# Four branch products of a decoder layer, eight half products each, rewritten as seven in Strassen's form

## The chip, the cores and the metric

One Trainium2 chip, one core. The time is the device time of one execution of the whole kernel in microseconds. TensorE is called PE, VectorE DVE, ScalarE ACT, GpSimd Pool, and the queue that issues most transfers SP, as the profile does.

## What is computed

One decoder layer on 1024 tokens with 1024 features. A norm and one wide input projection feed four branches: forgetting attention, a linear recurrence, stick-breaking attention and attention into a memory of 256 tokens. What this case is about comes after them:

```python
branches = jnp.stack([y_fox, y_lru, y_sb, y_mem], axis=2).astype(x.dtype)
gates = jax.nn.sigmoid(proj("gates").reshape(b, s, N_BRANCH, D_MODEL) + b_gate[l])
projected = jnp.einsum('bsnc,ncd->bsnd', branches, w_branch[l])
mixed = jnp.sum(gates * projected, axis=2)
x = x + mixed @ w_out[l]
```

Each branch has its own 1024 x 1024 weight; the four products of 1024 x 1024 x 1024 are gated, summed to `mixed`, and go through `w_out`. A gated MLP follows. All of it is float32.

## The kernel before, in words

**Precision.** PE multiplies in a rounded float32 format (F32R). So every operand is split in a high part (an ACT cast, line 131) and a low part (source minus high part, a DVE `tensor_tensor`, line 132, function `split`), and each product is three matmuls: high by high, high by low, low by high (`mm3`, lines 184 to 191). A matmul takes a 128 x 128 weight tile and a 128 x 512 operand.

**Before the branch products.** Norm and projections, the recurrence, then the attention stage, in which PE alternates between attention and a filler of projections by a planner's costs (lines 555 to 952). The filler's last work are the gate projections; they read the normed input `hTh`, `hTl` (64 KB of each partition) to their end, and their raw results go to DRAM (`gate_d`, without the sigmoid). The branches' results `y_d` lie in DRAM too. In the fox part of that stage Pool makes a sum of two 128 x 1024 tiles once per head (`fd`, line 745), and DVE splits projection weights there with line 132; in the stick-breaking part Pool masks 128 x 128 blocks with `affine_select` (line 832).

**The branch products (lines 957 to 1007).** The order is 1, 3, 0, 2 (recurrence, memory, fox, stick-breaking). For each branch the eight 128-row strips of `y_d[b]` are loaded (line 981) and split into twelve slots, so that strips of the next branch come in while this one is multiplied; the slots of the first branch lie outside the space of `hTh` and `hTl`. For every pair of output strips 256 columns of the weight are loaded and split by `load_w` (lines 210 to 228). For every output strip `m` the gate is loaded (line 990) and put through a sigmoid on ACT (line 991), 48 matmuls fill a PSUM tile of 128 x 1024, and DVE multiplies it by the gate (line 999 or 1001) and, from the second branch on, adds it to `mixed[m]` (line 1002). In the last branch `mixed[m]` is split at once (line 1005). Pool has nothing to do here.

**After.** The output projection takes the parts of `mixed` as weights, in 128 x 256 matmuls (lines 1018 to 1036), then the MLP.

The program is written in order, and a scheduler settles the order on every engine's queue and all waits; each engine and SP work their queues in order.

Of the kernel before, what the change touches and what calls it, by code (L numbers as in the profile page):

```python
# [7 lines left out]
F32 = mybir.dt.float32  # L8
F32R = mybir.dt.float32r
AF = mybir.ActivationFunctionType  # L10
ALU = mybir.AluOpType
AX = mybir.AxisListType
PSUM = bass.MemoryType.PSUM
DRAM = bass.MemoryType.DRAM

P = 128
S = 1024
D = 1024
KT = D // P
# [43 lines left out]
def build(tc, a, out):  # L63
    nc = tc.nc
# [17 lines left out]
    gate_d = dp.tile([4, D, S], F32, name="gate_d")  # L82
    y_d = dp.tile([4, D, S], F32, name="y_d")
# [46 lines left out]
    def split(src, hi, lo):  # L130
        nc.scalar.copy(hi, src)  # L131
        nc.vector.tensor_tensor(lo, src, hi, op=ALU.subtract)  # L132
# [42 lines left out]
    def pe(ins):  # L175

        if prev:
            tc.add_manual_dep(ins.ins, prev.pop().ins.name, NOSYNC, reason="order")
        prev.append(ins)
# [4 lines left out]
    def mm3(ps, pairs, pe=None):  # L184

        n = len(pairs)
        for i, (wh, wl, xh, xl) in enumerate(pairs):
            for j, (l, r) in enumerate(((wh, xh), (wh, xl), (wl, xh))):
                ins = nc.tensor.matmul(ps, l, r, start=(i == 0 and j == 0), stop=(i == n - 1 and j == 2))  # L189
                if pe:  # L190
                    pe(ins)
# [4 lines left out]
    pp = tc.alloc_tile_pool(name="psA", bufs=1, space=PSUM, reuse_waits="tile")  # L196
    hp = tc.alloc_tile_pool(name="hp", bufs=1, reuse_waits="tile")
    wp = tc.alloc_tile_pool(name="wp", bufs=2, side="right", reuse_waits="tile")
# [11 lines left out]
    def load_w(pool, src, n, step=None, gain=None):  # L210


        wh = pool.tile([P, KT, n], F32R, tag="wh", name="wh", bufs=2)
        wl = pool.tile([P, KT, n], F32R, tag="wl", name="wl", bufs=2)
        rk = 1024 // n
        for k0 in range(0, KT, rk):
            wr = pool.tile([P, rk, n], F32, tag="wr", name="wr", bufs=WRB)
            nc.sync.dma_start(wr, src[k0 * P:(k0 + rk) * P, :].rearrange("(k p) n -> p k n", p=P))
            if gain is not None:
                for k in range(rk):  # L220
                    g, h = gain[:, k0 + k:k0 + k + 1], wh[:, k0 + k, :]
                    nc.scalar.activation(h, wr[:, k, :], AF.Identity, scale=g)
                    nc.vector.scalar_tensor_tensor(wl[:, k0 + k, :], wr[:, k, :], g, h, op0=ALU.mult, op1=ALU.subtract)
                continue
            for k in range(0, rk, step or rk):
                ks, kd = slice(k, k + (step or rk)), slice(k0 + k, k0 + k + (step or rk))
                split(wr[:, ks, :], wh[:, kd, :], wl[:, kd, :])
        return wh, wl
# [22 lines left out]
    with ExitStack() as s1:  # L251
# [5 lines left out]
        def next_w(src, raw=None):  # L257
            wpools.reverse()
            return load_w512(wpools[1], src, raw)
# [108 lines left out]
        for name, base in (("fq", C_FQ), ("fk", C_FK), ("fv", C_FV), ("sv", C_SV), ("mq", C_MQ)):  # L368
            for c in range(0, D, 512):
                w = w_first if (name == "fq" and c == 0) else next_w(w_in[:, base + c:base + c + 512])  # L370
# [17 lines left out]
    with ExitStack() as s1:  # L388
# [77 lines left out]
        for c in range(KT):  # L466
# [3 lines left out]
            nxt = lru_in(c + 1) if c + 1 < KT else None  # L470
# [7 lines left out]
    with ExitStack() as s1:  # L478
# [3 lines left out]
        pp = s1.enter_context(tc.tile_pool(name="psA2", bufs=1, space=PSUM, reuse_waits="tile"))  # L482
# [433 lines left out]
        while vi < len(vq):  # L916
            now = clock["pe"] - (HOPF if vq[vi][0] in fox else HOP)
            if vi < ti:
                n, jp = vq[vi]
# [11 lines left out]
            if ti < len(vq) and ti - vi < PHB and slots["T"][-BANKS[1]] <= now:  # L931
                n, jp = vq[ti]
# [4 lines left out]
            if si < len(sq) and slots["S"][-BANKS[0]] <= now:  # L937
                n, f = sq[si]
# [15 lines left out]
    hp.release()  # L954


    pp = tc.alloc_tile_pool(name="psB", bufs=1, space=PSUM, reuse_waits="tile")
    xp = tc.alloc_tile_pool(name="xp", bufs=1, reuse_waits="tile")
    mixed = [xp.tile([P, S], F32, tag="x%d" % k, name="mixed") for k in range(KT)]
    ya = tc.alloc_tile_pool(name="ya", bufs=1, reuse_waits="tile")  # L960
    yb = tc.alloc_tile_pool(name="yb", bufs=1, side="right", reuse_waits="tile")

    def y_slot(g, k):
        n = (8 * g + k + 4) % 12
        pool = ya if n < 8 else yb
        return (pool.tile([P, S], F32R, tag="h%d" % n, name="yh"), pool.tile([P, S], F32R, tag="l%d" % n, name="yl"))

    def mmb():
        return pp.tile([P, 2, 512], F32, tag="up", name="mmb", bufs=3)

    def Tb():
        return pp.tile([P, 512], F32, tag="dn", name="T", bufs=2)

    order = (1, 3, 0, 2)
    mhl = []
    for g, b in enumerate(order):
        ys = {}
        ko = [4, 5, 6, 7, 0, 1, 2, 3] if g == 0 else list(range(KT))
        for k in ko:
            yr = yb.tile([P, S], F32, tag="yr", name="yr", bufs=2)  # L980
            nc.sync.dma_start(yr, y_d[b, k * P:(k + 1) * P, :])
            hl = y_slot(g, k)
            split(yr, *hl)
            ys[k] = hl
        for m in range(KT):
            if m % 2 == 0:
                w = load_w(wp, a["w_branch"][0, b, :, m * P:m * P + 256], 256)
            off = (m % 2) * P
            gt = yb.tile([P, S], F32, tag="gt", name="gt", bufs=2)
            nc.sync.dma_start(gt, gate_d[b, m * P:(m + 1) * P, :])  # L990
            nc.scalar.activation(gt, gt, AF.Sigmoid)
            ps = mmb()
            for half in range(2):
                sl = slice(half * 512, half * 512 + 512)
                mm3(ps[:, half], [(w[0][:, k, off:off + P], w[1][:, k, off:off + P], ys[k][0][:, sl], ys[k][1][:, sl])
                                  for k in ko])
            ps = ps.rearrange("p a n -> p (a n)")
            if g == 0:
                nc.vector.tensor_tensor(mixed[m], ps, gt, op=ALU.mult)
            else:  # L1000
                nc.vector.tensor_tensor(gt, ps, gt, op=ALU.mult)
                nc.vector.tensor_tensor(mixed[m], mixed[m], gt, op=ALU.add)
            if g == 3:
                hl = y_slot(4, m)
                split(mixed[m], *hl)
                mhl.append(hl)
    yb.release()

    hp = tc.alloc_tile_pool(name="h2", bufs=1, side="right", reuse_waits="tile")
    h2h = hp.tile([P, KT, S], F32R, name="h2h")  # L1010
# [9 lines left out]
    for t0 in (0, 4):  # L1020
        for c in range(0, D, 256):
            w = load_w(wp, a["w_out"][0, :, c:c + 256], 256)
            for t in range(t0, t0 + 4):
                sl = slice(t * P, (t + 1) * P)
                ps = mmb()[:, 0, :256]
                mm3(ps, [(mhl[k][0][:, sl], mhl[k][1][:, sl], w[0][:, k, :], w[1][:, k, :]) for k in range(KT)],
                    pe if c + 256 == D or turns else None)
                if len(turns) > 1 or (turns and c + 256 < D and t > t0):
                    turns.pop(0)(pe)
                    if not turns:  # L1030
                        prev.clear()
                nc.vector.tensor_tensor(x2[t][:, c:c + 256], x2[t][:, c:c + 256], ps, op=ALU.add)
                if c + 256 == D:
                    turns.append(norm_T(np_, Tb, x2[t], None, h2h, h2l, t * P, 1, mmb().rearrange("p a n -> p (a n)")))
# [17 lines left out]
    for p in range(NFF // 2):  # L1052
# [3 lines left out]
        al = tp.tile([P, 2, S], F32R, tag="al", name="al", bufs=2)  # L1056
        for f in range(2):
            n = 2 * p + f
# [10 lines left out]
        wh = tp.tile([P, 2, D], F32R, tag="dh", name="wdh")  # L1069
        wl = tp.tile([P, 2, D], F32R, tag="dl", name="wdl")  # L1070
        for f in range(2):
            wr = tp.tile([P, D], F32, tag="dr", name="wdr", bufs=2)
            nc.sync.dma_start(wr, wd[(2 * p + f) * P:(2 * p + f + 1) * P, :])
            split(wr, wh[:, f], wl[:, f])
        for t in range(NT):
            ts = slice(t * P, (t + 1) * P)
            for half in range(2):
                sl = slice(half * 512, half * 512 + 512)
                ps = pp.tile([P, 512], F32, tag="dn", name="dn", bufs=2)
# [4 lines left out]
    tp.release()  # L1084
    pp.release()
    hp.release()
    wp.release()
    xp.release()
    edge.release()
    es.close()  # L1090

# [25 lines left out]
```

## Time and profile before

| | us |
|---|---|
| median of 3 runs (2983.04 to 2988.02) | 2984.13 |
| the profiled execution's own time | 2983.88 |
| its span, from the first instruction to the last | 2982.2 |
| the stretch of the branch products, first to last matmul's start | 1799.42 to 2152.21 |
| end of the last split of `mixed` | 2158.46 |

The span lies inside the time of the same execution; the 1.7 us between them are around the program. Positions in the trace are counted from the span's start. "Granted clock" is TensorE's, 1.00 being 2.4 GHz. A matmul's duration in the trace is longer than the distance to the next one, as matmuls overlap; what a row of matmuls takes is read from their starts.

### The profile page before, as it was taken

To read this page: it belongs to the slowest core of one execution; us is meant where nothing else is said; L and a number is where in the kernel's file an instruction comes from. 1 tells how busy PE (TensorE), PEld (TensorE's weight loads), DVE (VectorE), ACT (ScalarE), POOL (GpSimd) and SP (SyncE) were. 2 spreads that over 40 slices of the span, in tenths; PEclk is the share of its full clock that TensorE was granted. 3 is DMA by queue.
4 is the path that set the end of the run, shared out by engine and by line. 5 is a ranking of instruction groups with operands and counts; after the bars stand their busy time and mean duration, and the time that the engine had idled before them with its cause. 6 is when DMAs were issued, how large, how long until landed. Compare 5 with 4: busy or idle time off the path is not lost. (4 is left out here: it accounts for less than half of the span.)

```text
span 2982.2 us, 38824 instructions
## 1 busy us (share of the span) xinstructions
PE 2913.9 (98%) x14800; PEld 2461.8 (83%) x14800; DVE 1737.7 (58%) x3261; ACT 1270.0 (43%) x2264; POOL 301.9 (10%) x502
## 2 busy tenths in 40 slices
PE   8999999999999999999999999999999999999999
PEld 6878888887888888888887888888898888888887
DVE  8564325556657877878888873443445444444443
ACT  5333223578346666666666662322234222222221
POOL 0000000000312122224433320000000000000000
PEclk9999999999999999999999999999999999999999
DMA  6345543212766566644444534443422111111101
GB/s 214 127 142 183 184 146 122 71 57 62 268 196 184 170 161 161 165 123 135 119 128 120 133 121 162 145 159 113 139 88 85 43 52 48 43 43 57 57 29 57
DMA packets 210922, 358.77 MB, mean 120 GB/s; under 512 B 14816, under 2 KB 141824, under 8 KB 206640
## 3 DMA queue, kind: packets, MB, share of 16 engines
q1 hardware_dynamic: 189744, 267.49, 27.8%
q0 software_dynamic: 20992, 88.79, 11.3%
q8 instruction: 117, 1.92, 0.3%
q14 instruction: 69, 0.57, 0.1%
HBM read 255.50 MB, written 100.73 MB: 119 GB/s over the span
## 5 line engine op out<-in xcount | busy, mean ns | idle before, releaser
L182 PE MATMUL mm<-hTl,wh 128*128 128x512 f32 x768 | 304.9, 397 | 0.0
L182 PE MATMUL mm<-hTh,wh 128*128 128x512 f32 x768 | 304.2, 396 | 0.7 <-DVE fs L589 0.7
L182 PE MATMUL mm<-hTh,wl 128*128 128x512 f32 x768 | 304.1, 396 | 0.0
L132 DVE TENSOR_TENSOR wl<-wr,wh 128x1024 fp32r<-128x1024 f32 (+1 forms) x216 | 209.5, 998 | 111.3 <-ACT wh L131 111.0
L189 PE MATMUL up<-h2h,wl 128*128 128x512 f32 x704 | 274.2, 389 | 0.0
L189 PE MATMUL up<-h2h,wh 128*128 128x512 f32 x704 | 274.1, 390 | 0.0
L189 PE MATMUL up<-h2l,wh 128*128 128x512 f32 x704 | 273.9, 389 | 0.0
L189 PE MATMUL mm<-wh,hTh 128*128 128x512 f32 x640 | 255.2, 399 | 2.2 <-ACT hTh L131 2.2
L131 ACT CAST wh<-wr 128x1024 fp32r<-128x1024 f32 (+1 forms) x216 | 176.7, 865 | 179.5 <-PE mmb L189 75.4
L189 PE MATMUL mm<-wh,hTl 128*128 128x512 f32 x640 | 251.3, 393 | 0.2 <-DVE hTl L132 0.2
L189 PE MATMUL mm<-wl,hTh 128*128 128x512 f32 x640 | 250.5, 391 | 0.0
L614 DVE TENSOR_TENSOR pl<-T,ph 128x512 fp32r<-128x512 f32 (+1 forms) x336 | 203.1, 632 | 66.8 <-ACT ph L613 65.8
L613 ACT CAST ph<-T 128x512 fp32r<-128x512 f32 (+1 forms) x336 | 172.7, 553 | 133.1 <-PE T L851 119.7
L182 PE MATMUL S<-kx,qq 128*128 128x512 f32 (+2 forms) x768 | 196.7, 357 | 8.5 <-DVE mx L802 7.2
L189 PE MATMUL mmb<-yh,wh 128*128 128x512 f32 x512 | 198.3, 390 | 2.7 <-ACT yh L131 2.7
L189 PE MATMUL mmb<-yl,wh 128*128 128x512 f32 x512 | 199.2, 390 | 0.3 <-DVE yl L132 0.3
L189 PE MATMUL mmb<-yh,wl 128*128 128x512 f32 x512 | 198.6, 389 | 0.0
L1081 DVE TENSOR_TENSOR x<-x,dn 128x512 f32<-128x512 f32 x176 | 119.9, 687 | 101.7 <-PE dn L189 101.7
L851 PE MATMUL T<-ident,pr 128*128 128x128 f32 x1152 | 162.4, 277 | 14.1 <-DVE pr L837 14.1
L834 DVE TENSOR_TENSOR_SCAN gm<-gm 128x128 f32<-128x128 f32 (+7 forms) x128 | 171.5, 1358 | 7.7 <-POOL gm L832 7.6
L182 PE MATMUL PV<-pl,vx 128*128 128x256 f32 (+1 forms) x640 | 159.8, 288 | 14.2 <-DVE pl L614 14.1
L182 PEld LDWEIGHTS mm<-hTh,wh 128*128 128x128 f32 x768 | 145.1, 189 | 26.4 <-DVE fs L589 1.1
(270 smaller groups left out, 6342.3 us busy)
## 6 DMA issues: line engine op xcount, KB each, us to landing
wr<-in_w_in_dram SPq DMA_DIRECT2D x104, 512.0 KB, 4.6
wr<-in_w_up_dram SPq DMA_DIRECT2D x44, 512.0 KB, 3.5
qq<-fq_d POOLq DMA_DIRECT2D x32, 512.0 KB, 7.1
gate_d<-gs SPq DMA_DIRECT2D x64, 256.0 KB, 2.4
qq<-sq_d POOLq DMA_DIRECT2D x32, 512.0 KB, 5.1
wr<-in_w_branch_dram SPq DMA_DIRECT2D x32, 512.0 KB, 4.8
yr<-y_d SPq DMA_DIRECT2D x32, 512.0 KB, 4.2
gt<-gate_d SPq DMA_DIRECT2D x32, 512.0 KB, 3.9
```

Source lines behind the costliest of these rows:

```text
L131: nc.scalar.copy(hi, src)
L132: nc.vector.tensor_tensor(lo, src, hi, op=ALU.subtract)
L182: pe(nc.tensor.matmul(*args, **kw))
L189: ins = nc.tensor.matmul(ps, l, r, start=(i == 0 and j == 0), stop=(i == n - 1 and j == 2))
L613: nc.scalar.copy(ph[:, :n], t[:, :n])
L614: nc.vector.tensor_tensor(pl[:, :n], t[:, :n], ph[:, :n], op=ALU.subtract)
L834: nc.vector.tensor_tensor_scan(gm[:, 0:w][:, ::-1], gm[:, 0:w][:, ::-1], gm[:, 0:w][:, ::-1], 1.0, op0=ALU.mult, op1=ALU.min)
L851: pe(nc.tensor.transpose(t[:, n * P:(n + 1) * P], self.prs[qi][:, j * P:(j + 1) * P], ident))
L1081: nc.vector.tensor_tensor(x2[t][:, sl], x2[t][:, sl], ps, op=ALU.add)
```

## The change

Per branch the weight and the branch's result are cut in halves both ways: `a11` to `a22` are 512 x 512 quarters of the weight (features by inputs), `b11` to `b22` of `y_d[b]` (inputs by tokens). Seven half products of 512 x 512 x 512 are made, 48 matmuls each: a11 b11, a12 b21, s1 t1, s2 t2, s4 b22, s3 t3 and a22 t4, where s1 to s4 and t1 to t4 are eight sums of quarters, made on Pool on tiles of 128 x 2048 (most of them in place of a quarter). Each product's two operands are split into parts just one product ahead (`prep`), in two buffers each: four casts on ACT and four 128 x 1024 subtractions on DVE per product. PSUM holds two sets of four banks, `al` and `be`; products that share a sum accumulate in one bank, and in between three of the seven are copied out by ACT (`kept`). `take` loads a 128 x 512 gate, puts it through the sigmoid, adds the copy to the bank on DVE, multiplies by the gate on DVE and adds to `mixed` on Pool (on DVE for the last product of the last branch). The raw quarters lie in `ya`, which is now where `hTh` and `hTl` were, and in `yb`; `mixed` moves to the other side of SBUF. Loads are four weight quarters and four quarters of `y_d`, 1 MB each, per branch, and 16 gates of 256 KB. For the next branch, a11 and b11 are asked for after the fourth product, a12 and b22 after the fifth, the other four after the sixth.

The diff, cut to its core:

```diff
+    xp = tc.alloc_tile_pool(name="xp", bufs=1, side="right", reuse_waits="tile")
+    ya = tc.alloc_tile_pool(name="ya", bufs=1, reuse_waits="tile")
+    yb = tc.alloc_tile_pool(name="yb", bufs=1, reuse_waits="tile")
+    def add(out_, a_, b_, op):
+        nc.gpsimd.tensor_tensor(out_, a_, b_, op=op)
+    LA, LB = (0, 1, 2, 3, 8), (4, 5, 6, 7, 9)
+    def parts(pool, src, tag):
+        h = pool.tile([P, 4, 512], F32R, tag=tag + "h", name=tag + "h", bufs=2)
+        l = pool.tile([P, 4, 512], F32R, tag=tag + "l", name=tag + "l", bufs=2)
+        for k in (0, 2):
+            split(src[:, k:k + 2], h[:, k:k + 2], l[:, k:k + 2])
+        return h, l
+    def prep(a_, b_):
+        return parts(wp, a_, "w") + parts(yb, b_, "y")
+    def product(bank, ops, first):
+        wh, wl, yh, yl = ops
+        for q in range(4):
...
+            for k in range(4):
+                for j, (l, r) in enumerate(((wh, yh), (wh, yl), (wl, yh))):
+                    nc.tensor.matmul(ps, l[:, k, fs], r[:, k], start=(first and k == 0 and j == 0),
+                                     stop=(k == 3 and j == 2), skip_group_check=not first)
+            yield q, ps
+    def take(g, q, i, l, ps, part):
+        gt = yb.tile([P, 512], F32, tag="gt", name="gt", bufs=5)
+        nc.sync.dma_start(gt, gate_d[b, m * P:(m + 1) * P, sl])
+        nc.scalar.activation(gt, gt, AF.Sigmoid)
+        if part is not None:
+            nc.vector.tensor_tensor(part, part, ps, op=ALU.add)
+            ps = part
+        if g == 0:
+            nc.vector.tensor_tensor(mixed[m][:, sl], ps, gt, op=ALU.mult)
+        else:
+            nc.vector.tensor_tensor(gt, ps, gt, op=ALU.mult)
+            eng = nc.vector if g == 3 and i == 1 and l == 0 else nc.gpsimd
+            eng.tensor_tensor(mixed[m][:, sl], mixed[m][:, sl], gt, op=ALU.add)
...
+    for g, b in enumerate(order):
+        add(s1, r["a21"], r["a22"], ALU.add)
+        add(t1, r["b12"], r["b11"], ALU.subtract)
+        cur, ops = ops, prep(r["a12"], r["b21"])
+        p1 = [kept(ps, "p1") for q, ps in product("al", cur, True)]
+        add(s3, r["a11"], r["a21"], ALU.subtract)
+        add(s2, s1, r["a11"], ALU.subtract)
+        add(t2, r["b22"], t1, ALU.subtract)
+        cur, ops = ops, prep(s1, t1)
+        for q, ps in product("be", cur, True):
+            take(g, q, 0, 0, ps, p1[q])
+        add(s4, r["a12"], s2, ALU.subtract)
+        add(t3, r["b22"], r["b12"], ALU.subtract)
+        cur, ops = ops, prep(s2, t2)
+        x5 = [kept(ps, "x5") for q, ps in product("be", cur, True)]
+        add(t4, r["b21"], t2, ALU.subtract)
+        cur, ops = ops, prep(s4, r["b22"])
+        u2 = [kept(ps, "u2") for q, ps in product("al", cur, False)]
+        cur, ops = ops, prep(s3, t3)
+        for q, ps in product("be", cur, False):
+            take(g, q, 0, 1, ps, u2[q])
+        cur, ops = ops, prep(r["a22"], t4)
+        for q, ps in product("al", cur, False):
+            take(g, q, 1, 1, ps, x5[q])
+        cur = ops
+        if b1 is not None:
+            ops = prep(nxt["a11"], nxt["b11"])
+        for q, ps in product("al", cur, False):
+            take(g, q, 1, 0, ps, None)
+            if b1 is None:
+                mixed_parts(4 + q)
-    yb = tc.alloc_tile_pool(name="yb", bufs=1, side="right", reuse_waits="tile")
...
-        for m in range(KT):
-            if m % 2 == 0:
-                w = load_w(wp, a["w_branch"][0, b, :, m * P:m * P + 256], 256)
-            off = (m % 2) * P
-            gt = yb.tile([P, S], F32, tag="gt", name="gt", bufs=2)
-            nc.sync.dma_start(gt, gate_d[b, m * P:(m + 1) * P, :])
-            nc.scalar.activation(gt, gt, AF.Sigmoid)
...
-            if g == 0:
-                nc.vector.tensor_tensor(mixed[m], ps, gt, op=ALU.mult)
-            else:
-                nc.vector.tensor_tensor(gt, ps, gt, op=ALU.mult)
-                nc.vector.tensor_tensor(mixed[m], mixed[m], gt, op=ALU.add)
```

`mixed_parts` splits a strip of `mixed` as line 1005 did; strips 0 to 3 after the fifth product of the last branch, 4 to 7 after the last product's quarters. In the first branch (`g == 0`) nothing is added to `mixed`.

## Rows read from the trace of the kernel before

**Rows 1.** The page's first part: busy time, share of span, instructions.

```profile
span 2982.2 us, 38824 instructions
PE 2913.9 (98%) x14800; PEld 2461.8 (83%) x14800; DVE 1737.7 (58%) x3261; ACT 1270.0 (43%) x2264; POOL 301.9 (10%) x502
```

**Rows 2.** Stretches: length, each engine's busy time and instructions, granted clock, DMA.

```profile
0.00:10.00 10.00, 1.38 (x7) 1.41 (x8) 2.37 (x9) 3.97 (x6) 3.21 (x11) 1.00 0.83 239
10.00:20.00 10.00, 7.89 (x26) 5.62 (x25) 8.58 (x17) 7.82 (x13) 0.00 (x0) 1.00 1.01 404
...
1799.40:2152.40 353.00, 350.03 (x1537) 287.38 (x1536) 143.35 (x121) 99.73 (x98) 0.00 (x0) 1.00 0.43 139
```

**Rows 3.** Timeline, PE, at the start of the branch products.

```profile
1799.19 0.39 PE L182 MATMUL mm<-hTh,wl 128*128 128x512 f32 x1
1799.42 0.39 PE L189 MATMUL mmb<-yh,wh 128*128 128x512 f32 x1
...
1801.91 0.39 PE L189 MATMUL mmb<-yh,wl 128*128 128x512 f32 x1
```

**Rows 4.** Groups by line of the same stretch, costliest first.

```profile
L189 PE MATMUL mmb<-yl,wh 128*128 128x512 f32 x512 | 199.2, 390 | 0.3 <-DVE yl L132 0.3
...
L189 PE MATMUL mmb<-yh,wh 128*128 128x512 f32 x512 | 198.3, 390 | 2.7 <-ACT yh L131 2.7
...
L132 DVE TENSOR_TENSOR wl<-wr,wh 128x1024 fp32r<-128x1024 f32 x32 | 38.6, 1218 | 12.0 <-ACT wh L131 12.0
...
L131 ACT CAST yh<-yr 128x1024 fp32r<-128x1024 f32 x28 | 29.0, 1049 | 37.0 <-DMA yr<-y_d 33.9 <-PE mmb L189 3.0
```

**Rows 5.** Timeline, DVE: two splits in a run; the last split of `mixed`.

```profile
1826.94 2.36 DVE L132 TENSOR_TENSOR wl<-wr,wh 128x1024 fp32r<-128x1024 f32 x2 [0.36 <-ACT wh L131]
...
2157.24 1.22 DVE L132 TENSOR_TENSOR yl<-mixed,yh 128x1024 fp32r<-128x1024 f32 x1
```

**Rows 6.** Groups by line, whole span: Pool's sum, and ACT on 128 x 512.

```profile
L745 POOL TENSOR_TENSOR fd<-fb,mask 128x1024 f32<-128x1024 f32 x16 | 38.6, 2409 | 87.4 <-DMA fb<-fb_d 68.1 <-DVE sm L821 13.7 <-DVE mx L671 5.7
...
L811 ACT ACTIVATE gm<-S 128x512 f32<-128x512 f32 x80 | 48.7, 609 | 39.7 <-DVE pr L837 26.1 <-PE S L182 8.1 <-POOL pr L832 4.4
```

**Rows 7.** Timeline, DVE then Pool, around the Pool sum at 934.89.

```profile
934.97 0.69 DVE L614 TENSOR_TENSOR pl<-T,ph 128x512 fp32r<-128x512 f32 x1 [0.65 <-ACT ph L613]
935.58 2.27 DVE L132 TENSOR_TENSOR wl<-wr,wh 128x512 fp32r<-128x512 f32 x1
...
934.89 2.40 POOL L745 TENSOR_TENSOR fd<-fb,mask 128x1024 f32<-128x1024 f32 x1 [6.01 <-DMA fb<-fb_d]
```

**Rows 8.** Timeline, DVE then Pool, around the Pool sum at 1159.19.

```profile
1160.33 3.62 DVE L132 TENSOR_TENSOR wl<-wr,wh 128x512 fp32r<-128x512 f32 x4 [0.40 <-ACT wh L131]
...
1159.19 2.40 POOL L745 TENSOR_TENSOR fd<-fb,mask 128x1024 f32<-128x1024 f32 x1 [6.17 <-DMA fb<-fb_d]
```

**Rows 9.** Line 132 from 900 to 1290: shortest, median, longest in ns.

```profile
L132 DVE TENSOR_TENSOR wl<-wr,wh x32: 672/682/2268, 935.6 to 1254.5; 128x512 fp32r<-128x512 f32 x32
```

**Rows 10.** Timeline, DVE then Pool, 1342 to 1347.

```profile
1342.61 0.77 DVE L132 TENSOR_TENSOR wl<-wr,wh 128x512 fp32r<-128x512 f32 x1
1343.30 1.21 DVE L837 TENSOR_TENSOR pr<-pr,gm 128x1023 f32<-128x1023 f32 x1
1344.44 1.88 DVE L132 TENSOR_TENSOR wl<-wr,wh 128x512 fp32r<-128x512 f32 x3
1346.24 0.68 DVE L614 TENSOR_TENSOR pl<-T,ph 128x512 fp32r<-128x512 f32 x1
...
1342.80 3.67 POOL L832 TENSOR_SCALAR_AFFINE_SELECT pr<-pr 128x128 f32<-128x128 f32 x1
1346.43 0.28 POOL L832 TENSOR_SCALAR_AFFINE_SELECT gm<-gm 128x128 f32<-128x128 f32 x1
```

**Rows 11.** DMA issues: size of each, median us from issue to landing.

```profile
wr<-in_w_branch_dram SPq DMA_DIRECT2D x32, 512.0 KB, 4.8
gt<-gate_d SPq DMA_DIRECT2D x32, 512.0 KB, 3.9
```

More of the change, by code (lines that the diff above doesn't have):

```diff
@@ L954, in build @@
     hp.release()
-    pp = tc.alloc_tile_pool(name="psB", bufs=1, space=PSUM, reuse_waits="tile")
-    xp = tc.alloc_tile_pool(name="xp", bufs=1, reuse_waits="tile")
+    pp = tc.alloc_tile_pool(name="psW", bufs=1, space=PSUM, reuse_waits="tile")
+    xp = tc.alloc_tile_pool(name="xp", bufs=1, side="right", reuse_waits="tile")
     mixed = [xp.tile([P, S], F32, tag="x%d" % k, name="mixed") for k in range(KT)]
     ya = tc.alloc_tile_pool(name="ya", bufs=1, reuse_waits="tile")
-    yb = tc.alloc_tile_pool(name="yb", bufs=1, side="right", reuse_waits="tile")
@@ L963, in y_slot, with raw @@
[L963 to L966, printed above, removed]
+    yb = tc.alloc_tile_pool(name="yb", bufs=1, reuse_waits="tile")
+    def raw(n, name):
+        return (ya if n < 8 else yb).tile([P, 4, 512], F32, tag="r%d" % n, name=name)
+    def add(out_, a_, b_, op):
+        nc.gpsimd.tensor_tensor(out_, a_, b_, op=op)
+    LA, LB = (0, 1, 2, 3, 8), (4, 5, 6, 7, 9)
@@ new lines, in load_a, with load_b @@
+    def load_a(b, i, j, slot):
+        t = raw(LA[slot], "wr%d%d" % (i, j))
+        nc.sync.dma_start(t, a["w_branch"][0, b, j * 512:(j + 1) * 512, i * 512:(i + 1) * 512].rearrange(
+            "(k p) n -> p k n", p=P))
+        return t
+    def load_b(b, j, l, slot):
+        t = raw(LB[slot], "yr%d%d" % (j, l))
+        nc.sync.dma_start(t, y_d[b, j * 512:(j + 1) * 512, l * 512:(l + 1) * 512].rearrange("(k p) n -> p k n", p=P))
+        return t
+    def parts(pool, src, tag):
[4 more added lines that the diff above has]
+        return h, l
@@ new lines, in prep @@
+    def prep(a_, b_):
[3 more added lines that the diff above has]
+        for q in range(4):
+            fs = slice(q * P, (q + 1) * P)
+            if first:
+                banks[bank, q] = pp.tile([P, 512], F32, tag="%s%d" % (bank, q), name=bank)
+            ps = banks[bank, q]
+            for k in range(4):
[3 more added lines that the diff above has]
+            yield q, ps
@@ new lines, in build, with kept @@
+    banks = {}
+    order = (1, 3, 0, 2)
+    mhl = [None] * KT
+    def kept(ps, name):
+        t = yb.tile([P, 512], F32, tag="ev", name=name, bufs=8)
+        nc.scalar.copy(t, ps)
+        return t
+    def take(g, q, i, l, ps, part):
+        b, m, sl = order[g], q + 4 * i, slice(l * 512, (l + 1) * 512)
+        gt = yb.tile([P, 512], F32, tag="gt", name="gt", bufs=5)
[10 more added lines that the diff above has]
+            eng.tensor_tensor(mixed[m][:, sl], mixed[m][:, sl], gt, op=ALU.add)
@@ new lines, in mixed_parts, with first_loads @@
+    def mixed_parts(m):
+        pair = mhl[m // 2 * 2]
+        if m % 2 == 0:
+            pair = (ya.tile([P, 2, S], F32R, tag="r%d" % MT[m // 2][0], name="mh"),
+                    ya.tile([P, 2, S], F32R, tag="r%d" % MT[m // 2][1], name="ml"))
+        split(mixed[m], pair[0][:, m % 2], pair[1][:, m % 2])
+        mhl[m] = pair
+    MT = ((0, 4), (1, 7), (2, 5), (3, 6))
+    def first_loads(b):
+        return {"a11": load_a(b, 0, 0, 0), "b11": load_b(b, 0, 0, 0)}
+    nxt = first_loads(order[0])
@@ new lines, in build @@
+    nxt.update(a12=load_a(order[0], 0, 1, 1), b21=load_b(order[0], 1, 0, 2))
+    nxt.update(a21=load_a(order[0], 1, 0, 2), a22=load_a(order[0], 1, 1, 3))
+    nxt.update(b12=load_b(order[0], 0, 1, 1), b22=load_b(order[0], 1, 1, 3))
+    ops = prep(nxt["a11"], nxt["b11"])
+    for g, b in enumerate(order):
+        r, nxt = nxt, {}
+        b1 = order[g + 1] if g < 3 else None
+        s1 = raw(LA[4], "s1")
+        add(s1, r["a21"], r["a22"], ALU.add)
+        t1 = raw(LB[4], "t1")
+        add(t1, r["b12"], r["b11"], ALU.subtract)
+        cur, ops = ops, prep(r["a12"], r["b21"])
+        p1 = [kept(ps, "p1") for q, ps in product("al", cur, True)]
+        s3, s2 = r["a21"], r["a11"]
+        add(s3, r["a11"], r["a21"], ALU.subtract)
+        add(s2, s1, r["a11"], ALU.subtract)
+        t2 = r["b11"]
+        add(t2, r["b22"], t1, ALU.subtract)
+        cur, ops = ops, prep(s1, t1)
+        for q, ps in product("be", cur, True):
+            take(g, q, 0, 0, ps, p1[q])
+        s4, t3 = r["a12"], r["b12"]
+        add(s4, r["a12"], s2, ALU.subtract)
+        add(t3, r["b22"], r["b12"], ALU.subtract)
+        cur, ops = ops, prep(s2, t2)
+        x5 = [kept(ps, "x5") for q, ps in product("be", cur, True)]
+        t4 = r["b21"]
+        add(t4, r["b21"], t2, ALU.subtract)
+        cur, ops = ops, prep(s4, r["b22"])
+        u2 = [kept(ps, "u2") for q, ps in product("al", cur, False)]
+        if b1 is not None:
+            nxt = first_loads(b1)
+        cur, ops = ops, prep(s3, t3)
+        for q, ps in product("be", cur, False):
+            take(g, q, 0, 1, ps, u2[q])
+        if b1 is not None:
+            nxt.update(a12=load_a(b1, 0, 1, 1), b22=load_b(b1, 1, 1, 3))
+        else:
+            for m in range(4):
+                mixed_parts(m)
+        cur, ops = ops, prep(r["a22"], t4)
+        for q, ps in product("al", cur, False):
+            take(g, q, 1, 1, ps, x5[q])
+        if b1 is not None:
+            nxt.update(b21=load_b(b1, 1, 0, 2), a21=load_a(b1, 1, 0, 2), a22=load_a(b1, 1, 1, 3),
+                       b12=load_b(b1, 0, 1, 1))
+        cur = ops
+        if b1 is not None:
+            ops = prep(nxt["a11"], nxt["b11"])
+        for q, ps in product("al", cur, False):
+            take(g, q, 1, 0, ps, None)
+            if b1 is None:
+                mixed_parts(4 + q)
@@ L968, in mmb @@
+    yb.release()
+    pp.release()
+    pp = tc.alloc_tile_pool(name="psB", bufs=1, space=PSUM, reuse_waits="tile")
     def mmb():
@@ L972, in Tb @@
         return pp.tile([P, 512], F32, tag="dn", name="T", bufs=2)
[L974 to L984, printed above, removed]
-        for m in range(KT):
-            if m % 2 == 0:
-                w = load_w(wp, a["w_branch"][0, b, :, m * P:m * P + 256], 256)
-            off = (m % 2) * P
-            gt = yb.tile([P, S], F32, tag="gt", name="gt", bufs=2)
-            nc.sync.dma_start(gt, gate_d[b, m * P:(m + 1) * P, :])
-            nc.scalar.activation(gt, gt, AF.Sigmoid)
[L992 to L997, printed above, removed]
-            if g == 0:
-                nc.vector.tensor_tensor(mixed[m], ps, gt, op=ALU.mult)
-            else:
-                nc.vector.tensor_tensor(gt, ps, gt, op=ALU.mult)
-                nc.vector.tensor_tensor(mixed[m], mixed[m], gt, op=ALU.add)
[L1003 to L1007, printed above, removed]
     hp = tc.alloc_tile_pool(name="h2", bufs=1, side="right", reuse_waits="tile")
@@ L1025, in build @@
                 ps = mmb()[:, 0, :256]
-                mm3(ps, [(mhl[k][0][:, sl], mhl[k][1][:, sl], w[0][:, k, :], w[1][:, k, :]) for k in range(KT)],
+                mm3(ps, [(mhl[k][0][:, k % 2, sl], mhl[k][1][:, k % 2, sl], w[0][:, k, :], w[1][:, k, :]) for k in range(KT)],
                     pe if c + 256 == D or turns else None)
@@ L1086, in build @@
     hp.release()
+    xp.release()
     wp.release()
-    xp.release()
     edge.release()
```

## The prediction

> **What bounds the kernel now.** I began with the page: PE is busy for 98% of the span, DVE for 58%, ACT for 43%, Pool for 10% [rows 1]. The table by stretches then says the same of the 353.0 us of the branch products: PE 350.0, DVE 143.4, ACT 99.7, Pool nothing at all, granted clock 1.00 [rows 2]. The list of groups by line gives the matmuls, three kinds of 512 each, 1536 in all [rows 4]. Their 0.39 us are overlapped; the timeline has eleven steps from 1799.42 to 1801.91, so one matmul takes 2.49 / 11 = 0.2264 us [rows 3]. 1536 x 0.2264 = 347.8 us: the stretch is matmuls back to back, with 5 us of stops. It begins with no pause behind the last gate matmul, which reads hTh [rows 3], and its last consequence, the last split of `mixed`, ends at 2157.24 + 1.22 = 2158.46 [rows 5]. From 1799.4 that is **359.1 us**, the figure that I set the new stretch against. The rest of the program is unchanged, so the sum is made on the profiled execution's own 2983.88 us, which is 0.25 below the median of the runs shown. Some 0.2% (6 us) is what a measurement of this kernel can tell from no change.
>
> **The change, part by part.**
>
> *PE.* 4 branches x 7 products x 48 = 1344 matmuls of the same shape: 192 fewer, worth 192 x 0.2264 = **43.5 us**, and 304.3 us are left. This is the whole gain, and it comes only if PE stays the bound.
>
> *DVE.* Parts used to be made once per operand strip, 16 splits of 128 x 1024 per branch. Now they are made per product: 7 x 2 x 2 = 28 per branch. In a run one takes 2.36 - 1.22 = 1.14 us [rows 5], so 112 x 1.14 = 127.7 us. A `take` with a kept copy costs an addition from PSUM and a multiplication by the gate, 12 per branch, at 128 x 512: in a run of three such splits, (1.88 - 0.68) / 2 = 0.60 us each [rows 10]. The multiplications with both operands in SBUF come to 48 x 0.60 = 28.8; the instructions that read a bank (48 additions and the 16 multiplications of the seventh products) to 38.4. The last branch has four additions to `mixed` (2.4) and eight splits of it (9.1). All told 206 us: by itself under PE's 304.
>
> *Pool.* Sums of 128 x 1024 took 2.41 us on average and 2.40 in the two that I follow below [rows 6 to 8]. Of 128 x 2048 and 128 x 512 the trace has none; I take 2.40 per 1024 in proportion. The other end is a fixed part as large as Pool's shortest mask, 0.28 [rows 10]: then a long sum is 0.28 cheaper and a short one (2.40 + 0.28) / 2 - 1.20 = 0.14 dearer, 32 x 0.28 - 44 x 0.14 = 3 us less in all. Eight sums of 2048 per branch are 64 units; additions to `mixed`, 16 quarters in the second and third branch and 12 in the last, are 22: 86 x 2.40 = **206.4 us**, also under 304. GPSIMD Engine Reference of the Trainium skill, section 3.1, gives 4497 ns for an addition of N = 2048 in float32, where proportion gives 4.80; by it the sum below would be 32 x 0.30 = 9.7 us less, near 3028; no run here shows that length.
>
> *DVE and Pool together.* Each fits beside PE, but the trace shows that they don't fit beside one another. At 934.89 Pool begins a sum and holds until 937.29. DVE, with a bank as one of its sources, isn't touched (0.69 us). Its next instruction is a split of `wl` from `wr` and `wh`, both in SBUF: started at 935.58, it takes 2.27 us and ends 0.56 after Pool's sum [rows 7]. The median of that instruction in the same stage is 0.682, and 2.268 is the longest of 32 [rows 9]. It happens again at 1159.19: four splits take 3.62 us where 0.68 + 3 x 0.60 = 2.48 is usual, 1.14 more, and Pool's sum still had 1.26 to run [rows 8]. So a DVE instruction with two SBUF sources does nothing while a Pool sum runs. The other way round too: a Pool mask of 0.28 us takes 3.67 us, while DVE runs five such instructions one behind the other, and it ends just after a DVE instruction with a bank as its source has begun [rows 10]. Splits, the multiplications of kept copies and the additions to `mixed` are all of this kind, and so are the Pool sums. They are one queue: 127.7 + 28.8 + 2.4 + 9.1 + 206.4 = **374.4 us**, against 304.3 of PE. Per branch it is 57.6 + 31.9 + 7.2 = 96.7 us in the second and third, against 76.1 of PE.
>
> *What the queue can't fill.* The operand buffers are two, so the parts of product n + 1 can't be begun before product n - 1 is done, and each time a cast of 1.05 us [rows 4] stands ahead of the first split. In that time the queue may be empty: between 0 and 28 x 1.05 = 29.4 us. I take 29.4, as no code prepares anything further ahead, and some parts wait for Pool's sum as well.
>
> *The start.* The raw quarters now lie in the space of hTh and hTl, free only at 1799.4; the first branch's slots used not to. Two loads of 1 MB at the best rate shown, 404 GB/s, are 5.2 us [rows 2], and a 512 KB load lands in 4.8 [rows 11], of which its bytes are 1.3 at that rate, so 3.5 are latency. a11's first split can begin at 3.5 + 2.6 + 1.05 = 7.2 us; b11 lands at 8.7, and its first cast and split end at 10.9, when the first matmul starts. For the common queue I take 9 us, between the two; bounds 6 and 14, the latter if the loads run at half that rate. The other six quarters land behind, 2.6 us each, while the queue works.
>
> *What is hidden.* ACT per branch: 28 casts x 1.05, and 28 copies and sigmoids at 0.61 [rows 6] make 46.5 of at least 76. DMA moves the same 12 MB per branch (a mean share of 0.43 in the stretch before [rows 2]), and SP issues 24 transfers per branch as before. The last four loads stand in the queue ahead of the seventh product's four gates (10.4 us at 404 GB/s, and 3.9 to land [rows 11]); these are wanted two products later, so I charge 0, at most 5 us at each of three branch ends, and only if PE is the bound. Copies (`kept`) and the first matmuls of the output projection cost nothing: the former are behind other products, the latter run on strips 0 to 3 until the last split, the same chain (multiply, add, cast, split) as before; bound +6. The clock was 1.00 even in the first 10 us, with PE busy for 1.38 [rows 2]; I charge nothing for PE's new waits.
>
> **Sum.** 9 + 374.4 + 29.4 = 412.8 us to the last split, against 359.1: +53.7. 2983.88 + 53.7 = 3037.6, so **3038 us**. With the empty time at 0, the start at 6 and Pool's fixed part, it would be 2983.9 + 53.7 - 29.4 - 3 - 3 = 3002.
>
> **The rivals.**
>
> *PE stays the bound (faster).* For it: only two DVE splits met a Pool sum in this trace, both of 128 x 512; nobody saw a queue of both. Against it: both were held to the Pool sum's end to within 0.6 us. If they ran side by side, the stretch would be 11 + 304.3 + 6.1 for the tail (2152.4 to 2158.5) + the 5 us of stops of before = 326, 33 less: 2951. This decides if the port is held for so little of a Pool sum that the common queue falls under PE's time: (304 - 168) / 206, two thirds of its duration. Chance 0.12. If the part held is a little above this, the time passes through no change on its way to 3038: 0.04.
>
> *Who goes first (slower still).* In rows 10 DVE kept the port through five instructions. If Pool does the same with s3, s2 and t2 in a row (14.4 us) and s4, t3 (9.6), DVE stands still with the split at its head, and the additions from banks behind it don't run beside Pool any more: up to 38.4 more, 3038 to 3076. If the two take turns instead, Pool gets in after every split, and the same bound holds. Rows 10 speak against turns: Pool asked at 1342.80, and four more DVE instructions went ahead. It decides from the point at which two Pool sums are ready at once. Chance 0.12. SBUF — State Buffer of the Trainium skill, section "Who interferes with whom", has the exclusive hold too and says that issue order decides who blocks; by that rule it would be turns, and this trace does not agree on that part.
>
> *The saving isn't there.* That the change does not drop 192 matmuls can be set aside: the loops of the diff give 48 per product and seven products per branch, without a condition.
>
> **How the numbers follow.** The forecast has 0.72, the rival of turns 0.12, side by side 0.12, between 0.04. Faster by over 0.2%: 0.13; within: 0.04; slower: 0.83. The range runs from 2996, the first case with every bound at its low end (3002) and a measurement's grain of 6 under it, to 3080, the second at its end (3076) with most of the tail's bound; it leaves out side by side, the case between and little more.
>
> **What would show it.** Right: PE stops for 5 to 20 us in products that wait for s1, s2, s4 or their parts; 128 x 1024 splits with 2 to 6 us among ones of 1.22; DVE and Pool together near full through the stretch; 1344 matmuls at 0.226. Wrong: splits at 1.22 throughout beside Pool sums, PE busy share near 95% in the stretch and its length near 320. A stop of about 11 us at 1799 is there in either case.

## The result, and the profile after

The changed kernel takes 3050.98 us (median of 4 runs, 3049.19 to 3054.01) against 2983.59 for the kernel before: ratio 1.0226, 95% interval 1.0208 to 1.0243. It is slower by 67 us (62 to 73); 54 were forecast. The profiled execution took 3054.01, 70.1 more than that of before.

The page of the changed kernel, its first part:

```profile
span 3052.2 us, 38870 instructions
PE 2897.8 (95%) x14608; PEld 2441.1 (80%) x14608; DVE 1930.1 (63%) x3369; ACT 1342.7 (44%) x2392; POOL 551.0 (18%) x578
```

192 matmuls are gone, as said, and the span is 70 us longer: PE now waits. Against [rows 1] DVE is busy for 192 us more and Pool for 249 more. The table of stretches shows where (columns as in [rows 2]); the bounds are the last gate matmul, the four branches' ends in round figures, and the tail:

```profile
1799.40:1809.30 9.90, 0.04 (x1) 0.04 (x1) 2.42 (x3) 3.63 (x5) 0.00 (x0) 0.74 0.95 316
1809.30:1906.00 96.70, 75.08 (x288) 58.83 (x288) 79.66 (x42) 41.94 (x54) 56.41 (x11) 0.85 0.47 169
1906.00:1998.00 92.00, 79.73 (x336) 64.52 (x336) 80.55 (x57) 42.14 (x56) 51.45 (x16) 0.95 0.41 137
1998.00:2102.00 104.00, 83.15 (x336) 67.40 (x336) 85.07 (x56) 41.69 (x56) 71.04 (x24) 0.89 0.36 122
2102.00:2219.00 117.00, 96.04 (x387) 77.49 (x388) 98.10 (x78) 49.13 (x65) 68.86 (x26) 0.89 0.24 77
```

336 matmuls, a branch's share, took 92 and 104 us where back to back they would be 76. DVE is busy for over 80% of each, Pool for more than half, and much of both is waiting: that is seen in the groups by line of the stretch (behind the count: busy us in all, mean ns of one, then the engine's idle us before them and what ended them).

```profile
L132 DVE TENSOR_TENSOR wl<-wr,wh 128x1024 fp32r<-128x1024 f32 x52 | 107.4, 2091 | 73.2 <-ACT wh L131 72.9
...
L132 DVE TENSOR_TENSOR yl<-yr,yh 128x1024 fp32r<-128x1024 f32 x48 | 97.7, 2076 | 3.1 <-ACT yh L131 3.1
L1031 POOL TENSOR_TENSOR mixed<-mixed,gt 128x512 f32<-128x512 f32 x44 | 82.6, 1900 | 104.9 <-DVE gt L1029 104.9
...
L132 DVE TENSOR_TENSOR wl<-s,wh 128x1024 fp32r<-128x1024 f32 x8 | 29.4, 3718 | 21.2 <-ACT wh L131 21.2
...
L1024 DVE TENSOR_TENSOR u<-u,be 128x512 f32<-128x512 f32 x16 | 10.6, 683 | 3.3 <-PE be L1004 3.3
```

The split that took 1218 ns in [rows 4] takes 2091 on average, and 3718 where its source is a sum. The addition from a bank (line 1024) takes 683, and no longer beside Pool than without it (683 in experiment 1 too). By shortest, median and longest (line 132 first, then the sums of quarters):

```profile
L132 DVE TENSOR_TENSOR wl<-wr,wh x52: 1210/1226/5653, 1805.9 to 2224.5; 128x1024 fp32r<-128x1024 f32 x52
```

```profile
L969 POOL TENSOR_TENSOR wr<-wr,wr x8: 4612/5436/5508, 1824.3 to 2142.7; 128x2048 f32<-128x2048 f32 x8
...
L969 POOL TENSOR_TENSOR wr<-s,wr x4: 5409/5524/5552, 1834.4 to 2123.7; 128x2048 f32<-128x2048 f32 x4
```

Of all 124 splits of 128 x 1024 in the stretch (four of them for `w_out`) 22 took over 4 us; what splits took over 1.222 each comes to 115.9 us in all. The timeline of Pool and DVE in the first branch shows how:

```profile
1834.38 5.51 POOL L969 TENSOR_TENSOR wr<-s,wr 128x2048 f32<-128x2048 f32 x1
1839.85 5.52 POOL L969 TENSOR_TENSOR yr<-yr,t 128x2048 f32<-128x2048 f32 x1
1845.33 5.51 POOL L969 TENSOR_TENSOR wr<-wr,wr 128x2048 f32<-128x2048 f32 x1
1850.80 9.99 POOL L969 TENSOR_TENSOR yr<-yr,yr 128x2048 f32<-128x2048 f32 x2
```

```profile
1835.42 0.68 DVE L1024 TENSOR_TENSOR p<-p,be 128x512 f32<-128x512 f32 x1
1836.02 10.42 DVE L132 TENSOR_TENSOR yl<-t,yh 128x1024 fp32r<-128x1024 f32 x2
1846.37 5.02 DVE L1027 TENSOR_TENSOR mixed<-p,gt 128x512 f32<-128x512 f32 x1
1851.31 1.27 DVE L1024 TENSOR_TENSOR p<-p,be 128x512 f32<-128x512 f32 x2
1852.50 8.83 DVE L1027 TENSOR_TENSOR mixed<-p,gt 128x512 f32<-128x512 f32 x2
```

One Pool sum (4.6 us, and 0.9 of waiting), one DVE instruction with two SBUF sources, one Pool sum, and so on: turns. Behind a split at the head of DVE's queue stand the instructions that read banks, so the banks are not free for the next product. That is what PE mostly waits for (its waits in the stretch: us in total, times, longest):

```profile
PE al L1004 <- DVE x L1024: 24.1, 4, 9.0
PE be L1004 <- DVE p L1024: 22.0, 5, 7.1
PE al L1004 <- DVE gt L1029: 17.0, 2, 8.7
PE al L1004 <- ACT yh L131: 10.1, 1, 10.1
PE be L1004 <- DVE yl L132: 8.8, 4, 4.3
```

The 10.1 are the start; 63 of the rest are for banks, 9 for parts.

### The profile page after: what moved, and what is told of

The parts are those of the page before. It is cut to its first block, busy times and chain, and to the rows that moved or that the text cites. A ratio compares the mean times of both kernels' runs of the same rounds, so it can differ in the third digit from the quotient of the medians.

```text
span 3052.2 us, 38870 instructions
## 1 busy us (share of the span) xinstructions
PE 2897.8 (95%) x14608; PEld 2441.1 (80%) x14608; DVE 1930.1 (63%) x3369; ACT 1342.7 (44%) x2392; POOL 551.0 (18%) x578
## 5 line engine op out<-in xcount | busy, mean ns | idle before, releaser
L132 DVE TENSOR_TENSOR wl<-wr,wh 128x1024 fp32r<-128x1024 f32 (+1 forms) x232 | 273.0, 1206 | 174.3 <-ACT wh L131 173.5
L131 ACT CAST wh<-wr 128x1024 fp32r<-128x1024 f32 (+1 forms) x232 | 193.2, 876 | 187.4 <-PE mmb L189 44.3
L182 PEld LDWEIGHTS mm<-hTh,wl 128*128 128x128 f32 x768 | 144.9, 189 | 24.8
L182 PEld LDWEIGHTS mm<-hTl,wh 128*128 128x128 f32 x768 | 144.9, 189 | 24.4
L182 PE MATMUL PV<-ph,vx 128*128 128x256 f32 (+1 forms) x640 | 160.2, 278 | 0.0
```

The lines of the kernel that those rows point to most:

```text
L182: pe(nc.tensor.matmul(*args, **kw))
```

## The experiments

Each stands against the kernel before, which ran again beside it (2981 to 2982.4), and against the changed kernel's 3051 from the runs above. Ratios are to the kernel before, with 95% intervals.

**1. Pool as busy, but without the reads of the sums.** The sums of quarters are left out of the result; fills take their place. The 44 additions to `mixed` stay on Pool and do read.

```diff
-        nc.gpsimd.tensor_tensor(out_, a_, b_, op=op)
+        nc.gpsimd.memset(out_, 0.0)
+        nc.gpsimd.memset(out_, 0.0)
+        nc.gpsimd.memset(out_[:, 0:2], 0.0)
```

> Each of the 32 sums of quarters on Pool is replaced by fills of the same tile with zero, two of the whole tile and one of half of it (a fill of 128x1024 took 0.95 us, so 4.8 us, as long as a sum); Pool stays as busy, but reads nothing. The sums are left out of the result. Shared port (my theory): a Pool instruction that reads nothing doesn't hold DVE's second source, so the splits go back to 1.22 us, what is left of the common queue (168 + 53 us) is under PE's 304, and the time comes to 2950 to 2975. Rival, Pool is just too slow and its length sits in the chain of products: Pool is as long as before, so the time stays within 15 us of the changed kernel, 3035 to 3055. Rival, the halved TensorE clock behind PE's pauses is the cause, whatever makes the pauses: between the two, as the pauses shrink only where data are late.

2961.22 us, ratio 0.993 (0.9913 to 0.9947): 90 us less than with the sums. Groups by line of the stretch:

```profile
L132 DVE TENSOR_TENSOR wl<-s,wh 128x1024 fp32r<-128x1024 f32 x8 | 9.8, 1226 | 20.6 <-ACT wh L131 20.6
```

```profile
L970 POOL MEMSET yr<- 128x2048 f32 x12 | 21.9, 1822 | 0.2
L969 POOL MEMSET yr<- 128x2048 f32 x12 | 21.8, 1816 | 1.4 <-DVE yl L132 1.4
...
L971 POOL MEMSET yr<- 128x1024 f32 x12 | 11.6, 963 | 0.4
```

Three fills are 1.82 + 1.82 + 0.96 = 4.6 us, an unhindered sum's length, and stand at the sum's place in Pool's queue, ahead of the casts that read the tile. Yet the split of `s` is back from 3718 to 1226 ns, and no split is over 2.4 us. So neither Pool's length nor its place in the chain costs the 90 us; that its sums read SBUF does. (A fill doesn't wait for the sources that a sum has besides its own tile, as the loads of the quarters behind `s` and `t`; what this alone is worth was not run.)

**2. The sums on DVE.**

```diff
-        nc.gpsimd.tensor_tensor(out_, a_, b_, op=op)
+        nc.vector.tensor_tensor(out_, a_, b_, op=op)
```

> The 32 sums of quarters are made on DVE in place of Pool, everything else as in the changed kernel. Shared port: a sum of 128x2048 costs DVE 2048/960 + 0.07 = 2.2 us in place of 4.8 on the common queue; DVE is busy for 206 + 70 = 277 us, the common queue 168 + 70 + 53 = 291, both under PE's 304, so PE is nearly the bound again: 2960 to 2990. Rival, DVE is already too full (its busy time more than doubled in this stretch) and more work on it makes it worse: over 3060.

2981.49 us, ratio 0.9995 (0.9986 to 1.0005): level with the kernel before. More work on the busier engine is 70 us faster than the changed kernel. The additions to `mixed` left on Pool now take 2355 ns on average, against 1283 at the shortest in the changed kernel, and two of them 11.4 us: they are the ones that wait.

**3. The additions to `mixed` on DVE, the sums on Pool.**

```diff
-            eng = nc.vector if g == 3 and i == 1 and l == 0 else nc.gpsimd
+            eng = nc.vector
```

> The 40 additions to mixed that the changed kernel makes on Pool are made on DVE, the sums of quarters stay on Pool. Shared port: each leaves 1.2 to 2.3 us of Pool's on the common queue and puts 0.6 there, so 44 quarters less 4 that were on DVE already give some 26 us less at the shortest: 3010 to 3030. Rival, DVE too full: 24 us more of DVE's time, 3065 to 3075.

3036.61 us, ratio 1.018 (1.0165 to 1.0195): 14 less than the changed kernel, in the direction of the common queue but half the size, and 7 above the range that I gave. The edit moved 44 additions and not 40, as the expectation's first sentence has it.

**4. No sums at all.** The sums are left out of the result, and `s1`, `t1` stand for `a22`, `b12`.

```diff
-        nc.gpsimd.tensor_tensor(out_, a_, b_, op=op)
+        pass
-        s1 = raw(LA[4], "s1")
+        s1 = r["a22"]
-        t1 = raw(LB[4], "t1")
+        t1 = r["b12"]
```

> The 32 sums of quarters are left out altogether; the products take the unsummed quarters, so the result lacks them. Everything else as in the changed kernel. Shared port: 221 us of common queue under 304 of PE: 2945 to 2970, and the same as with the fills to within 10 us. Rival, Pool's length in the chain: the same 2945 to 2970 here, but not with the fills. If the start behind hTh and the loads at the branch ends are what costs, they stay: over 2980 here.

2953.7 us, ratio 0.9906 (0.9891 to 0.992), 8 under the fills. This is about what 1344 matmuls with all splits give when PE is the bound: behind the start PE has one pause over 1 us. The forecast's rival had worked out 2951.

**5. Sums and additions on DVE** (the edits of 2 and 3 together).

> Sums of quarters and additions to mixed both on DVE; Pool does nothing in the stretch. Shared port: with the sums on DVE the additions on Pool still took 2.36 us each and DVE's splits up to 1.49; without them DVE runs unblocked, 277 + 24 = 301 us against 304 of PE. 2970 to 2985, no worse than with the sums alone on DVE (2981). Rival, DVE too full: 20 us or more above that, over 3000.

2964.44 us, ratio 0.994 (0.9926 to 0.9954): **faster than both kernels**, though by 0.6% only over the kernel before; 17 below experiment 2 and better than I expected. The groups of the stretch have DVE's splits at their own length again:

```profile
L132 DVE TENSOR_TENSOR wl<-wr,wh 128x1024 fp32r<-128x1024 f32 x50 | 59.8, 1228 | 57.5 <-ACT wh L131 57.5
L132 DVE TENSOR_TENSOR yl<-yr,yh 128x1024 fp32r<-128x1024 f32 x48 | 56.7, 1227 | 3.1 <-ACT yh L131 3.1
L1031 DVE TENSOR_TENSOR mixed<-mixed,gt 128x512 f32<-128x512 f32 x48 | 31.4, 693 | 0.0
```

**6 to 8. The start.** In the changed kernel the first load is issued at 1799.16, and the first product begins 10.3 us behind the last gate matmul. I gave the first two quarters the slots outside the space of `hTh`, in the changed kernel (6), with the sums on DVE (7), and with all on DVE (8):

```diff
-    LA, LB = (0, 1, 2, 3, 8), (4, 5, 6, 7, 9)
+    LA, LB = (8, 1, 2, 3, 0), (9, 5, 6, 7, 4)
```

> The changed kernel with a11, b11 in the two raw slots that lie outside the space of hTh and hTl (8 and 9), and s1, t1 in slots 0 and 4; so the first two loads and their parts need not wait for the last gate matmul. Nothing else differs. If the start costs what the prediction priced (9 to 11 us of empty queue) it goes, and with it the stretch at half clock behind it: 10 to 16 us less than the changed kernel, 3035 to 3041. Rival, the common queue is behind anyway and the start is hidden in it: no change, 3048 to 3053.

> The sums of quarters on DVE and the first two quarters outside the space of hTh and hTl. Both parts as above: 2981 less 8 to 14, so 2966 to 2974, which would be faster than the kernel before. Rival, DVE is the bound here (309 us of the stretch with the waits) and the start is hidden by it: 2978 to 2983.

> As the one before, and the additions to mixed on DVE too. If freeing the shared port of the additions is worth more than DVE's 24 us, it is the fastest of the four, 2958 to 2970; otherwise 2970 to 2985.

3056.57 us (1.0251, 1.0237 to 1.0265), 2982.17 (1.0003, 0.9995 to 1.0012) and 2967.78 (0.9949, 0.9935 to 0.9963): nothing gained in any of them, and number 6 came out 6 us above the changed kernel, over both of its ranges. SP's timeline of number 6 shows why:

```profile
1775.14 22.13 SPq L595 DMA_DIRECT2D gate_d<-gs  x5
1801.62 0.38 SPq L975 DMA_DIRECT2D wr<-in_w_branch_dram  x1
1802.39 0.32 SPq L595 DMA_DIRECT2D gate_d<-gs  x1
1802.76 0.42 SPq L981 DMA_DIRECT2D yr<-y_d  x1
```

The loads still stand behind five gate stores in SP's queue and are no earlier. These runs tell nothing on what an earlier start would be worth.

**9 and 10. The start again,** with the pools laid out as before (`xp` left, `yb` right, the slots as in 6), in the changed kernel (9) and with all on DVE (10):

```diff
-    xp = tc.alloc_tile_pool(name="xp", bufs=1, side="right", reuse_waits="tile")
+    xp = tc.alloc_tile_pool(name="xp", bufs=1, reuse_waits="tile")
-    yb = tc.alloc_tile_pool(name="yb", bufs=1, reuse_waits="tile")
+    yb = tc.alloc_tile_pool(name="yb", bufs=1, side="right", reuse_waits="tile")
```

> The changed kernel with the pools laid out as in the kernel before (mixed under ya on one side, yb on the other) and a11, b11 in the two slots of yb: their loads now stand ahead of four of the last gate stores in SP's queue, where in the trial with slots 8 and 9 alone they stood behind. The stop before the first product (10.3 us) goes, with the slow matmuls behind it (2.7 us): 3036 to 3044 if that time is on the path of the common queue. Rival: the queue of DVE and Pool is what sets the end and begins with the sums, whose quarters still land after 1799: 3046 to 3053.

> The same layout with all sums and additions on DVE, where PE is nearly the bound: the stop of 10.4 us goes, and 2.7 us of slow matmuls: 2964 less 7 to 13, 2951 to 2957. If DVE is the bound there: 2960 to 2966.

In both the first product now follows the last gate matmul without a pause (timeline of PE, number 9):

```profile
1796.99 0.39 PE L182 MATMUL mm<-hTh,wl 128*128 128x512 f32 x1
1797.22 0.39 PE L1004 MATMUL al<-yh,wh 128*128 128x512 f32 x1
```

Number 9 takes 3047.45 us (1.0218, 1.0202 to 1.0233), which is the rival's range: of 10.3 us of pause at most 3.5 come back at the end, and its interval overlaps that of the changed kernel. PE's later pauses (over 0.7 us from one matmul's start to the next) grew from 79 to 88 us, which fits a common queue that sets the end. Number 10 takes **2959.2** (0.9927, 0.9915 to 0.994), the fastest that makes the whole result, some 5 below number 5; the intervals of the two overlap. It lies between its two ranges and decides for neither.

**11. Pool sums that no product needs.** All on DVE, and idle additions on Pool.

```diff
+        for k in range(7):
+            o = out_[:, k // 2, k % 2 * 256:k % 2 * 256 + 256]
+            nc.gpsimd.tensor_tensor(yb.tile([P, 256], F32, tag="idle", name="idle", bufs=1), o, o, op=ALU.add)
```

> All sums and additions on DVE, and besides Pool makes, behind each of the 32 sums, seven additions of 128x256 of the finished sum to itself into a scratch tile that nobody reads (7 x 0.7 = 4.9 us, as long as a sum on Pool; one buffer of 1 KB). No product waits for Pool. Shared port: the common queue is 264 us of DVE and 157 of Pool, 421, over PE's 304, so 3030 to 3075 in place of 2964. Rival, Pool cost only because products waited for it: 2960 to 2972.

3049.06 us, ratio 1.0227 (1.0213 to 1.0241), 85 above number 5 and in the range that I gave, but it is not the clean test that I meant. Pool's queue fell behind, and the loads of the next branch waited for the tiles that it still had to read. One group of its additions by shortest, median and longest, and SP's own waits:

```profile
L972 POOL TENSOR_TENSOR idle<-s x28: 613/1476/18522, 1822.1 to 2159.1; 128x256 f32<-128x256 f32 x28
```

```profile
SPq L978 <- POOL idle L972: 65.9, 6, 32.6
SPq L984 <- POOL idle L972: 35.8, 8, 7.3
```

So products did wait for Pool here, through the loads; three of PE's pauses took 16 to 19 us. Idle Pool reads cost about as much here as the useful ones did, but in part by another way, so that the time fell in my range is partly luck. Experiment 1 is the one that tells.

**12. Half of the sums.** `t1` to `t4` on DVE (a fifth argument of `add`), `s1` to `s4` on Pool.

```diff
-        add(t1, r["b12"], r["b11"], ALU.subtract)
+        add(t1, r["b12"], r["b11"], ALU.subtract, nc.vector)
```

> t1 to t4 on DVE, s1 to s4 and the additions to mixed on Pool: half of the sums moved. Shared port: 16 x (4.8 - 2.2) = 42 us less on the common queue, 374 to 332, still over 304: 2995 to 3020, between the changed kernel (3051) and all sums on DVE (2981). Rival, the chain of Pool sums: it is s1, s3, s2, s4 then, 19 us per branch in place of 38, no longer than the products that hide it, so the whole of the loss goes: 2965 to 2985.

3027.81 us, ratio 1.0157 (1.0143 to 1.0171): 23 below the changed kernel. The chain of Pool sums is half as long and most of the loss is still there; the time is 8 above the range that the queue gave me. Ten splits over 4 us are left of 22.

## Why the prediction was right, and where its sum was short

**The bound.** Right: PE gave way to DVE and Pool as one queue. Experiment 1 shows it against Pool's length, 12 against the chain, and 2 and 5 against DVE's load. PE's saving was real as well: without Pool's sums it comes out as 18 to 29 us under the kernel before (5 and 4), not as the full 43.5.

**The sum.** In the changed kernel's stretch I took every DVE instruction with two SBUF sources and every Pool addition, and joined their times: 366.0 us out of 427.9, from the last gate matmul to the last split of `mixed`. The queue had been priced at 374.4, so that term held to 2%. A long sum alone takes 4.6 us, not 4.80; the additions to `mixed` 1.28, not 1.20, at the shortest.

**What was too small is the time that the queue doesn't fill:** 427.9 - 366.0 = 62 us in place of 9 + 29.4. In 45 of it neither engine worked, 7 more than the 38.4 priced. In 16.5 DVE worked alone, with banks as sources, which the prediction had charged nothing, as such instructions can run beside Pool. With the 8.4 that the queue was shorter this makes the 15 us by which the stretch exceeds the 412.8. Two steps of the prediction can stand behind it; no run separates them.

- "I charge nothing for PE's new waits" was wrong as a statement on the clock. The granted clock was 1.00 in the stretch before [rows 2] and 0.85 to 0.95 in the branches now; behind most pauses TensorE runs for a while at its lower level, 1.2 GHz. The longest such stretch (columns as above):

```profile
1838.30:1855.40 17.10, 8.79 (x19) 6.03 (x20) 17.10 (x6) 5.96 (x8) 17.10 (x4) 0.50 0.06 16
```

  In all, the distances of matmuls between 0.3 and 0.7 us, most of them in those stretches, make 25.5 us more than 0.226 each; in experiment 4 it is 2.7. How much of that is on the path was not isolated by a run: the pauses come from the queue, and what removes them removes both.

- "This trace does not agree" on turns was right for that trace and hasty as a forecast. The mask of [rows 10] was passed by five DVE instructions, but the sums of the changed kernel come in after each one, as the timeline above shows. SBUF — State Buffer of the Trainium skill says in "Who interferes with whom" that issue order decides who blocks; the sums agree with that (5.5 us in place of 4.6), the mask and some additions of number 11 (up to 18.5 us in place of 0.6) don't. So the rival of turns is part of what happened: bank reads behind a blocked split ran late, and some of them alone. Its bound was 38 us more, and the time came 13 above the forecast.

**The start** was right in length (10.3 us to the first matmul, 10.9 said; a slow first product behind it). Its price doesn't stand by itself: 9 us were charged as queue time; with the pause gone (9) the time falls by 3.5 at most, as other empty time takes its place. **Signs.** Splits of up to 5.65 us and a matmul pitch of 0.226 outside the slow stretches came as said. PE's stops came too, but behind the start only 7 of 16 are over 5 us and none over 9.4, and they wait for banks more than for the parts of s1, s2 and s4.

**The rivals.** Side by side fell with the 22 long splits. Its price, 2951, is what number 4 came to within 3 us.

## What to carry to other kernels

Before work is moved to Pool, count the DVE instructions that read two SBUF tensors: with Pool's reads they were one queue here, and an idle Pool was no free engine. The same sums on the busier DVE (2.3 us in place of 4.6) turned a loss of 2.3% into no change, and with the additions to `mixed` on DVE too into a gain of 0.6%. And a saving in matmuls has to leave the next engine under the new, shorter PE time: the common queue, 374 us by the prediction, stood against 304 of PE.

## What the runs showed of the hardware that was not expected

- Pool fills and DVE instructions with two SBUF sources run side by side (1226 ns per split beside 4.6 us of fills), Pool additions and the same instructions don't (up to 5653).
- Which one goes first isn't always the same: the mask of before waited through five DVE instructions (3.67 us), the sums of 128 x 2048 got in after each one (0.9 us of waiting). Number 11 has both with additions of 128 x 256 that take 0.61 us alone: some got in after one DVE instruction and made it 0.4 us longer (a split 1.63 us in place of 1.22), and four waited 18.2 to 18.5 us, through 12 to 15 DVE instructions that kept their own length. Why was not tried.
- Around most pauses of PE the granted clock fell to half (1.2 GHz) for 3.4 to 17.1 us at a time, in the changed kernel at twelve places of the stretch, where the kernel before had none. Not around each: at a pause of 3.8 us at 1921 it stayed at 1.00.
